# First stage of a hybrid decoder block: the modulation's weight sums as row sums on VectorE, with new step durations and margins in the kernel's own planner

## The chip, the core and the metric

The kernel runs on one core of one Trainium2 chip. The metric is the device time of one execution in microseconds (us), as the median of several runs of the same program; lower is better. The profile is one more execution with the hardware profiler on; its own device time was 1111.09 us.

## What is computed

The reference is one decoder block over a sequence of 1024 tokens with 1024 channels, all in float32. A vector `c` gives six modulation vectors of 1024 each (`mod`). The normalised input is scaled and shifted by two of them, projected to queries, keys and values, and goes through two kinds of attention side by side: mixer A, a sliding window with a sink, and mixer B, a mixture of three dilated windows. The result is projected back, gated and added; then follows an MLP with 4096 hidden channels and a squared ReLU.

```python
cond = jax.nn.silu(c)
mod = (cond @ w_ada[l] + b_ada[l]).astype(x.dtype)
sh_a, sc_a, gt_a, sh_m, sc_m, gt_m = [m[:, None, :] for m in jnp.split(mod, N_MOD, axis=-1)]

h = rms_norm(x, g_attn_pre[l]) * (1 + sc_a) + sh_a
proj = h @ w_in[l]                       # 1024 x 2304: q, k, v of both mixers
...                                      # rotary turn of the first 16 channels of each head
oa = banded_attention(qa, ka, va, A_WINDOW - 1, sink=sink_a[l])
ob = dilated_mixture_attention(qb, kb, vb)
mixed = jnp.concatenate([rms_norm(oa, g_mix_a[l]), rms_norm(ob, g_mix_b[l])], axis=-1)
y = mixed @ w_out[l]
x = x + gt_a * rms_norm(y, g_attn_post[l])

h = rms_norm(x, g_mlp_pre[l]) * (1 + sc_m) + sh_m
y = jnp.square(jax.nn.relu(h @ w_up[l])) @ w_down[l]
x = x + gt_m * rms_norm(y, g_mlp_post[l])
```

## The kernel before

**Arithmetic.** Every float32 product is made of three passes on TensorE in a rounded format: each operand is split into a high part (a copy, on ScalarE, ACT) and a low part (the original less the high part, on VectorE, DVE), and high by high, low by high and high by low are added in PSUM. So each 128x512 product step is three matmuls (L897, L898, L900 in the projections; L1799 to L1801 in the output; L2232 to L2234 in the MLP).

**The planner.** The order of all work is set while the program is built. Each piece of work is a step with a duration written in the source, the steps it depends on, the buffers it takes and gives back, and a priority. The class `Sched` keeps a clock for each of PE (TensorE), ACT, DVE, POOL (GpSimd) and SP (the DMA queue), and again and again emits the step that can start first by its own durations (`pick`, `first` and `run`, L266 to L333). The queue of each engine is then fixed in that order, whatever the chip does. A step of a higher `crit` may overtake. On TensorE, steps stand in named streams ("dense" for projections, "s", "t" and "pv" for the attention's scores, transposes and products, "post", "mod", "xt" and so on); `prefer` (L2390) lists the streams by rank, and the first stream is taken whose head is ready `SURE` microseconds before now (L155, L311). Before the change that margin is 0 for the attention's streams. Durations come from small formulas such as `t_ps(n)` (ACT from PSUM), `t_sb(n)` (ACT from SBUF) and `t_dv(n)` (DVE, L338 to L363) with constants added by hand.

**First stage (L488 to L754).** Eight blocks of `x` (128 tokens x 1024, 512 KB each) are loaded, squared and summed on ACT (`x_block`, L635), the reciprocal root is taken on POOL (L479, L481), and each block is multiplied by it (L639 ACT or L640 DVE). Each block is transposed on TensorE at once (L647), and ACT or DVE copy the eight 128x128 pieces into `xnT` (L651). The first 2048 columns of `w_ada` (8 MB) arrive as four groups of four tiles (`load_ada`, L527). DVE adds up each group with the values of `silu(c)` as per-partition scalars into a 128x512 accumulator (`mod_group`, L667 and L669), TensorE sums it over partitions by 128x1 matmuls with ones (L677), and L683 to L685 make the scale `g_a` and shift `s_a` of two channel blocks k. Then, for each k, ACT writes the high part (L706) and the full value in place (L703), and DVE the low part (L709) into `hw` (`mod_chunk`). There are eight channel blocks of 128, and two token halves x of 512.

**First projection unit (`first_unit`, L919).** The columns of `w_in` are dealt to six units; each unit has three column blocks c. Unit 0 is computed while the first stage still runs: six accumulators (`acc`, one for each x and c) are held open, and k advances as the channel blocks come; the last two k (from `AHEAD` = 6) come accumulator by accumulator, so that each can be read out in turn. Until the fourth accumulator is opened, `filler` (L907) puts matmuls on constant ones (L914) into planned idle time of TensorE. The weights come in six tiles of 256 KB for each unit, split by ACT (L561) and DVE or POOL (L566).

**Rotary tables.** DVE reduces the angles (`f_turns`, L612 to L623), ACT takes the sines (`f_sin`, L627 and L628, with a table load on each side), POOL lays them out in rows (L729 and L735), TensorE transposes them (L741), ACT scales them (L743). `evac` turns an accumulator into queries and keys (L779 to L788, L796, L799) and values (L847, L853, L861, L864).

**Attention and output.** Units 1 to 5 follow ("dense" steps on `pj`) with the attention items of the earlier units between them: scores (L1311, L1156, L1216), minimum and exponent (L1326 and L1331 and their like), transposes (L1368, L1467), products (L1403, L1502). Meanwhile POOL sums the other columns of `w_ada` (L1045 to L1050). Then eight output blocks (`out_block`, L1698) load the attention's result `o`, split it (L1741 ACT, L1742 DVE), project it, norm it and transpose it for the MLP. `front` (L1713) is run in two parts for the first two blocks, which overlap the end of the attention.

**MLP.** Seven products in place of eight (a Strassen scheme) for each of four column parts, 2688 matmuls in a row.

## Time and profile before

| what | value |
|---|---|
| median of three runs | 1109.82 us (1108.37 to 1112.75) |
| profiled execution: its own time | 1111.09 us |
| profiled execution: span from first to last instruction | 1109.3 us |
| DVE, ACT, POOL busy | 816.1, 634.2, 270.5 us |
| matmuls on TensorE | 5280 |
| first MLP matmul starts | 486.1 us |
| last MLP matmul starts | 1099.0 us |

Times in the profile are microseconds from the span's start. A busy time of TensorE counts each matmul from its start to its modelled end; matmuls overlap, so the pitch from one start to the next says more than the duration of one. "Idle before" is the time that an engine stood still ahead of an instruction, with what ended it. The views used are the page, the busy time by windows, the order of time by engine, the groups by line and shape, and the waits.

### The profile page before, as it was taken

What the parts mean: (1) busy time and instruction counts of PE and PEld (TensorE: products, weight loads), DVE (VectorE), ACT (ScalarE), POOL (GpSimd) and SP (SyncE); (2) the same over time, 40 slices, a digit from 0 to 9 for tenths busy, and PEclk for the clock granted to TensorE, in tenths of its full rate; (3) what the DMA queues carried; (4) which work ended last, traced back from release to release, by engine and by line L of the source; (5) the groups of instructions that cost most, each with busy time, mean ns of one, the idle gap of its engine ahead of it and who ended that gap; (6) DMA issues with size and microseconds to landing.
All of it is one profiled execution on the core that took longest, in us unless ns stands there. A gap on an engine that the chain in (4) does not pass through costs nothing.

```text
span 1109.3 us, 15373 instructions
## 1 busy us (share of the span) xinstructions
PE 1085.2 (98%) x5280; PEld 901.6 (81%) x5280; DVE 816.1 (74%) x1442; ACT 634.2 (57%) x1161; POOL 270.5 (24%) x365
## 2 busy tenths in 40 slices
PE   8999999999999999999999999999999999999996
PEld 6778888888888888788888888888888888888885
DVE  6968776667767778679797654898644996537998
ACT  7859776655456857677675244743155632347542
POOL 2447767587566641100000000000000000000002
PEclk9999999999999999999999999999999999999999
DMA  9665556453525537547731379322576043593104
GB/s 332 195 211 169 152 182 214 141 197 115 194 75 197 176 107 246 171 184 269 276 143 58 130 248 349 136 76 75 197 268 228 1 133 115 191 329 143 58 1 152
DMA packets 93631, 189.56 MB, mean 171 GB/s; under 512 B 8560, under 2 KB 33264, under 8 KB 93552
## 3 DMA queue, kind: packets, MB, share of 16 engines
q1 hardware_dynamic: 93552, 188.57, 49.3%
q8 instruction: 42, 0.69, 0.3%
q14 instruction: 37, 0.30, 0.1%
HBM read 139.25 MB, written 30.41 MB: 153 GB/s over the span
## 4 chain that ended last, share of the span: by engine, by line
PE 79%; DVE 8%; POOL 3%; issue 3%; ACT 3%; DMA 3%; SPq 1%; DVEq 0%; POOLq 0%; ACTq 0%
PE mlp_ps L2233 17%; PE mlp_ps L2234 17%; PE mlp_ps L2232 17%; PE pj L897 4%; PE pj L900 3%; PE pj L898 3%; PE y_ps L1799 2%; PE y_ps L1801 2%; PE y_ps L1800 2%; PE s_ps L1216 1%; PE o_ps L1502 1%; PE o_ps L1403 1%; PE s_ps L1311 1%; POOL ada_acc L1050 1%; PE pt_ps L1467 1%
## 5 line engine op out<-in xcount | busy, mean ns | idle before, releaser
L2232 PE MATMUL mlp_ps<-hw 128*128 128x512 f32 x896 | 349.6, 390 | 0.0
L2234 PE MATMUL mlp_ps<-hw 128*128 128x512 f32 x896 | 348.6, 389 | 0.0
L2233 PE MATMUL mlp_ps<-hw 128*128 128x512 f32 x896 | 348.6, 389 | 0.0
L2232 PEld LDWEIGHTS mlp_ps<-hw 128*128 128x128 f32 x896 | 168.2, 188 | 35.3 <-issue 0.5
L2233 PEld LDWEIGHTS mlp_ps<-hw 128*128 128x128 f32 x896 | 168.2, 188 | 35.3 <-issue 0.5
L2234 PEld LDWEIGHTS mlp_ps<-hw 128*128 128x128 f32 x896 | 168.2, 188 | 34.9
L2000 DVE TENSOR_TENSOR hw<-w,hw 128x1024 fp32r<-128x1024 f32 x94 | 112.3, 1221 | 94.0 <-ACT hw L1993 93.7
L1993 ACT CAST hw<-w 128x1024 fp32r<-128x1024 f32 x94 | 95.5, 1049 | 129.8 <-PE mlp_ps L2234 93.1
L2332 POOL TENSOR_TENSOR st<-st,nhalf 128x1 f32<-128x1 f32 x8 | 7.8, 983 | 610.2 <-DVE st L2330 610.2
L897 PE MATMUL pj<-hw,w_hl 128*128 128x512 f32 x240 | 102.7, 428 | 2.0 <-ACT vt L847 2.0
L900 PE MATMUL pj<-hw,w_hl 128*128 128x512 f32 x240 | 94.7, 395 | 0.0
L898 PE MATMUL pj<-hw,w_hl 128*128 128x512 f32 x240 | 94.5, 394 | 0.0
L1993 ACT CAST hw<-u 128x1024 fp32r<-128x1024 f32 x48 | 48.7, 1052 | 64.5 <-PE mlp_ps L2234 64.5
L2000 DVE TENSOR_TENSOR hw<-u,hw 128x1024 fp32r<-128x1024 f32 x48 | 57.1, 1220 | 18.2 <-ACT hw L1993 18.2
L2290 DVE TENSOR_TENSOR yacc<-yacc,mlp_ps 128x512 f32<-128x512 f32 x96 | 62.2, 683 | 3.3 <-PE mlp_ps L2234 3.3
L1050 POOL TENSOR_TENSOR ada_acc<-ada_acc,wa_st 128x512 f32<-128x512 f32 x42 | 55.5, 1321 | 3.5
L900 PEld LDWEIGHTS pj<-hw,w_hl 128*128 128x128 f32 x240 | 45.2, 188 | 10.4
L1799 PE MATMUL y_ps<-hw,oh 128*128 128x512 f32 x128 | 51.9, 405 | 0.4 <-ACT y_sb L1817 0.4
L897 PEld LDWEIGHTS pj<-hw,w_hl 128*128 128x128 f32 x240 | 45.4, 189 | 6.0 <-ACT vt L847 2.2
L1800 PE MATMUL y_ps<-hw,oh 128*128 128x512 f32 x128 | 49.9, 390 | 0.0
L898 PEld LDWEIGHTS pj<-hw,w_hl 128*128 128x128 f32 x240 | 45.7, 190 | 3.8 <-issue 0.2
L2271 ACT ACTIVATE u<-u 128x512 f32<-128x512 f32 x48 | 29.0, 625 | 32.9 <-DVE u L2269 32.4
(257 smaller groups left out, 1992.8 us busy)
## 6 DMA issues: line engine op xcount, KB each, us to landing
hw<-s_dram SPq DMA_DIRECT2D x84, 512.0 KB, 4.2
wa_st<-in_w_ada SPq DMA_DIRECT2D x32, 512.0 KB, 4.6
w<-in_w_up SPq DMA_DIRECT2D x32, 512.0 KB, 4.7
w<-in_w_down SPq DMA_DIRECT2D x32, 512.0 KB, 7.1
s_dram<-hw SPq DMA_DIRECT2D x28, 512.0 KB, 3.7
qt<-hl SPq DMA_DIRECT2D x40, 256.0 KB, 2.5
w_st<-in_w_in SPq DMA_DIRECT2D x36, 256.0 KB, 2.9
x_sb<-in_x SPq DMA_DIRECT2D x16, 512.0 KB, 5.7
```

Source lines behind the costliest of these rows:

```text
L897: T.matmul(ps, w[:, 0, n], h[0], start=(k == 0), stop=False)
L898: T.matmul(ps, w[:, 1, n], h[0], start=False, stop=False)
L900: T.matmul(ps, w[:, 0, n], h[1], start=False, stop=(k == KC - 1))
L1050: G.tensor_tensor(ada.acc[:, :512], ada.acc[:, :512], wa[:, j], ALU.add)
L1799: T.matmul(ps[:], oh, wh[:, c0:c0 + 512], start=(k == 4 * m), stop=False)
L1800: T.matmul(ps[:], oh, wl[:, c0:c0 + 512], start=False, stop=False)
L1993: A.copy(out[j][0], flat(src[j]))
L2000: V.tensor_tensor(out[j][1], flat(src[j]), out[j][0].bitcast(F32), ALU.subtract)
L2232: T.matmul(ps[m][:], sh, mh, start=starts and k == 0, stop=False, **kw)
L2233: T.matmul(ps[m][:], sh, ml_, start=False, stop=False, **kw)
L2234: T.matmul(ps[m][:], sl, mh, start=False, stop=k == 3, **kw)
L2290: e = op("DVE", t_dv(512), lambda: V.tensor_tensor(y(), y(), ps[m][:], ALU.add), [e, ml.e_y[tb, n]], gives=gives, prio=1)
```

## The change

Four things are changed.

1. **The first stage.** The host hands over the first 2048 columns of `w_ada` a second time, transposed (`w_mod`: for each channel block k and each of shift and scale, 128 output channels on partitions by 1024 inputs). `silu(c)` is spread to all partitions: DVE makes a diagonal, TensorE sums it with ones (two matmuls), the result `condb` is copied to SBUF. Each element of `g_a` and `s_a` is then one row sum on DVE: 16 `tensor_tensor_reduce` of 128x1024 take the place of the accumulation and of the 128x1 matmuls. The blocks of `x` stay in eight buffers of their own; they are transposed only when channel block k is wanted, four token blocks at a time, and ACT reads high part and full value straight from PSUM. `xnT` and its copies are gone. The loads are in another order: four blocks of `x`, the two tiles of k = 0, a tile of `w_in`, the other four blocks of `x`, and then two tiles for each k. From x block 4 on DVE may do the square as well. The sine's table is loaded at the start, the exponent's after k = 2.
2. **Durations.** Some thirty durations in the planner's steps are set anew, most of them longer.
3. **Margins.** `SURE` is 0.3 for the attention's streams and "post". The last `xn` of one output block waits for that of the block before.
4. **First output blocks.** The split of `o` of blocks 0 and 1 has `crit` 1, and the two loads of one block stand in order.

```diff
-SURE = dict(s=0.0, t=0.0, pv=0.0, post=0.0, fin=1.0)
+SURE = dict(s=0.3, t=0.3, pv=0.3, post=0.3, fin=1.0)
...
+    w = inputs["w_ada"][0][:, :2 * D].reshape(P, KC, 2, KC, P)
+    h["w_mod"] = np.ascontiguousarray(w.transpose(3, 2, 4, 1, 0)).reshape(KC, 2, P, D)
...
 def t_ps(n):
-    return 0.055 + 0.00083 * n
+    return 0.12 + 0.00083 * n
 def t_sb(n):
-    return 0.098 + 0.00083 * n
+    return 0.16 + 0.00083 * n
...
-    order0 = [("x", 0), ("x", 1), ("x", 2), (0, 0), (0, 1), ("x", 3), (0, 2), ("w", 0), (0, 3), ("w", 1)]
+    order0 = [("x", 0), ("x", 1), ("x", 2), ("x", 3), (0, 1), (0, 0), ("w", 0)]
     order0 += [("x", t) for t in range(4, TB)]
+    for k in range(1, KC):
+        order0 += [(k, 1), (k, 0)] + {1: [("w", 1)], 2: [("w", 2)], 3: [("w", 3)], 4: [("w", 4)], 5: [("w", 5)]}.get(k, [])
...
+    e_sin = op("ACT", 1.5, lambda: A.activation(small.tile([P, 8], F32, name="rs_t", tag="rs_t")[:, 0:1], ones[:, 0:1],
+                                                AF.Sin), [e, e_init], prio=0)
...
+        V.tensor_tensor(by_k(bc["diag"]), ident.unsqueeze(1).to_broadcast([P, KC, P]),
+                        cond[:].unsqueeze(2).to_broadcast([P, KC, P]), ALU.mult)
...
+            T.matmul(bc[n][:], ones[:], bc["diag"][:, 512 * n:512 * n + 512], start=True, stop=True)
...
+        def dot(i, dst):
+            w = wa_t[k, i][:]
+            V.tensor_tensor_reduce(w, w, condb[:], 1.0, bb[:, k, i:i + 1], ALU.mult, ALU.add, dst[:, k:k + 1])
...
-                        V.scalar_tensor_tensor(b["acc"][:], w, cj, b["acc"][:], ALU.mult, ALU.add)
...
-                    T.matmul(b["ps"][:, k, i:i + 1], b["acc"][:, GW * i + k * P:GW * i + k * P + P], ones[:, 0:1],
-                             start=True, stop=True)
...
+        bank, tag, r_b = (px, "x", r_x) if half else (pt, "t", r_t)
+            for j in range(4):
+                T.transpose(b["ps"][:, j], x_t[4 * half + j][:, ks], ident)
+        eh = op("ACT", t_ps(512) + AP_COST, lambda: A.activation(hh, b["ps"][:], AF.Identity, bias=s_a[:, k:k + 1],
+                                                                    scale=g_a[:, k:k + 1]), [d] + e_ada[k], prio=0)
+            A.activation(b["h"][:], b["ps"][:], AF.Identity, bias=s_a[:, k:k + 1], scale=g_a[:, k:k + 1])
+        e = op("DVE", t_dv(512), lambda: V.tensor_tensor(hl, b["h"][:], hh.bitcast(F32), ALU.subtract), [eh, e],
+               gives=[(r_h, 1)], prio=0)
...
-            e = op("POOL", 4.0, f_rows, [e_rope], takes=[(r_place, 1)], prio=0)
+            e = op("POOL", 8.0 if r_place is r_wa else 4.4, f_rows, [e_rope], takes=[(r_place, 1)], prio=0)
...
-        e = op("DVE" if eng is V else "POOL", 1.2 if eng is V else 3.64, f_acc,
+        e = op("DVE" if eng is V else "POOL", 1.4 if eng is V else 4.1, f_acc,
...
-        e = op("DVE", 0.2, f_z, ex, prio=0)
+        e = op("DVE", 0.62, f_z, ex, prio=0)
...
-            el = load(f_lo, 262144 * n, deps, takes=[] if m0 else [(r_o_, 1)], prio=-8.5 if tb == 0 else -6)
+            el = load(f_lo, 262144 * n, deps + eo.get("ld", []), takes=[] if m0 else [(r_o_, 1)],
+                      prio=-8.5 if tb == 0 else -6)
+            eo["ld"] = [el]
...
-            e = op("ACT", t_sb(512 * n), f_oh, [el], takes=[(r_g[m0], n)], prio=2)
+            e = op("ACT", t_sb(512 * n), f_oh, [el], takes=[(r_g[m0], n)], prio=2, crit=int(early))
```

How this moves the queues is seen at three places. The first is TensorE from the program's first matmul on: `acc<-ones_r` are fillers, `pxt<-head,x_sb` the transposes of `x`, `acc<-hw,w_hl` the first real projections. Before:

```order
L914 MATMUL acc<-ones_r 128x512 x26
L647 MATMUL pxt<-head,x_sb 128x128 x8
L914 MATMUL acc<-ones_r 128x512 x2
L647 MATMUL pxt<-head,x_sb 128x128 x8
L914 MATMUL acc<-ones_r 128x512
L647 MATMUL pxt<-head,x_sb 128x128 x8
L914 MATMUL acc<-ones_r 128x512 x10
L647 MATMUL pxt<-head,x_sb 128x128 x8
L914 MATMUL acc<-ones_r 128x512 x3
L677 MATMUL pm<-ones,acc_a 128x1 x4
L914 MATMUL acc<-ones_r 128x512 x5
L897 MATMUL acc<-hw,w_hl 128x512
```

TensorE from the same place in the changed kernel (`pbc` is the spread of `silu(c)`):

```order
L909 MATMUL acc<-ones_r 128x512 x15
L609 MATMUL pbc<-diag,ones 128x512
L909 MATMUL acc<-ones_r 128x512
L609 MATMUL pbc<-diag,ones 128x512
L909 MATMUL acc<-ones_r 128x512 x25
L691 MATMUL pxt<-head,x_sb 128x128 x4
L909 MATMUL acc<-ones_r 128x512 x8
L892 MATMUL acc<-hw,w_hl 128x512
L893 MATMUL acc<-hw,w_hl 128x512
L909 MATMUL acc<-ones_r 128x512
```

Ahead of the first real matmul stood 32 transposes and four 128x1 matmuls (and 47 fillers); now four transposes, two `pbc` and 49 fillers stand there, and the other transposes come between the projections. In the whole program there are 61 fillers in place of 60, 64 transposes of `x` as before, and no `pm`.

The second place is DVE in the middle of the first stage. Before, two channel blocks came at a time, after a run of accumulations:

```order
L709 TENSOR_TENSOR hw<-xnT,hw 128x8x128 x2
L669 SCALAR_TENSOR_TENSOR acc_a<-wa,cond,acc_a 128x512 x4
L683 TENSOR_TENSOR g_a<-pm,bb 128x2
L684 TENSOR_TENSOR g_a<-g_a,head 128x2
L685 TENSOR_TENSOR s_a<-pm,bb 128x2
L669 SCALAR_TENSOR_TENSOR acc_a<-wa,cond,acc_a 128x512 x2
L566 TENSOR_TENSOR w_hl<-w_st,w_hl 128x512
```

DVE in the changed kernel, where `ISA wa,g_a<-wa,condb,bb` is one row sum and the row after it reads its accumulator:

```order
L672 ISA wa,g_a<-wa,condb,bb 128x1024
L672 ISA g_a 128x1
L676 TENSOR_TENSOR g_a<-g_a,head 128x1
L700 TENSOR_TENSOR hw<-h,hw 128x4x128 x2
L563 TENSOR_TENSOR w_hl<-w_st,w_hl 128x512
L672 ISA wa,s_a<-wa,condb,bb 128x1024
L672 ISA s_a 128x1
```

Each channel block now has two row sums of its own, and the low parts (L700, before L709) stand between them in pieces of half the size.

The third place is ACT around the first copy of values of unit 1, `vt<-pj` (`p_sb,den` are the attention's exponents, `ph<-pt_ps` copies of transposed probabilities, `otmp` copies of an attention result). Before:

```order
L1331 ACTIVATE p_sb,den_1258<-p_sb,mn_1257 128x257 x4
L1331 ACTIVATE p_sb,den_1323<-p_sb,mn_1322 128x257 x2
L796 ACTIVATE hl<-pj 64x512
L1331 ACTIVATE p_sb,den_1323<-p_sb,mn_1322 128x257 x2
L1438 COPY otmp<-o_ps 64x512
L1375 CAST ph<-pt_ps 128x512 x2
L847 COPY vt<-pj 64x512
L561 CAST w_hl<-w_st 128x512
```

ACT around the same copy in the changed kernel:

```order
L1326 ACTIVATE p_sb,den_1166<-p_sb,mn_1165 128x257 x2
L1370 CAST ph<-pt_ps 128x512 x2
L1326 ACTIVATE p_sb,den_1166<-p_sb,mn_1165 128x257 x2
L791 ACTIVATE hl<-pj 64x512
L1433 COPY otmp<-o_ps 64x512
L842 COPY vt<-pj 64x512
L1370 CAST ph<-pt_ps 128x512 x2
L1326 ACTIVATE p_sb,den_1288<-p_sb,mn_1287 128x257
```

Between `hl<-pj` and `vt<-pj` five instructions stood before, two exponents among them; now it is one.

More of the change, by code (lines that the diff above doesn't have):

```diff
@@ L117, in _host @@
     h["consts"] = c
-    return h
+    return {n: h[n] for n in _INS + ["consts"]}
 def _constants(c):
@@ L714, in hybrid_block @@
     for tb in range(TB):
         x_block(tb)
-    for g in range(4):
-        mod_group(g)
-    e = op("ACT", 3.2, f_sin, [e_ang] + e_xn[0] + e_xn[1], prio=8)
-    e_rope = op("DVE", 0.15, lambda: V.tensor_scalar(sinw[:, :, 0], sinw[:, :, 1], -1.0, None, ALU.mult), [e],
-                prio=8)
+    for k in range(KC):
+        ada_chunk(k)
+    for k, half in [(k, x) for k in range(KC) for x in range(2)]:
+        if half == 0 and k < 6:
+            split_w(0, k)
+        mod_chunk(k, half)
@@ L1193, in part @@
             return f
-        eq = op(("ACT", "POOL"), (t_as(1024), 1.5), (part(A.copy), part(G.tensor_copy)), e_q[u, 1], takes=[(r_qf, 1)],
+        eq = op(("ACT", "POOL"), (2.0, 2.03), (part(A.copy), part(G.tensor_copy)), e_q[u, 1], takes=[(r_qf, 1)],
                 prio=3)
```

213 lines of the change are left out of this document (94 added, 119 removed).

## Prediction

> **What bounds the kernel now.** I read the page first, for who is last.
>
> ```profile
> PE 1085.2 (98%) x5280; PEld 901.6 (81%) x5280; DVE 816.1 (74%) x1442; ACT 634.2 (57%) x1161; POOL 270.5 (24%) x365
> PE 79%; DVE 8%; POOL 3%; issue 3%; ACT 3%; DMA 3%; SPq 1%; DVEq 0%; POOLq 0%; ACTq 0%
> ```
>
> TensorE (PE) is busy in 98% of the span and carries 79% of the chain that ended last. So a change pays only where PE stands still, or runs matmuls that compute nothing. The busy time by windows (PE, PEld, DVE, ACT and POOL in us, granted clock, DMA share, GB/s) shows where that is.
>
> ```profile
> 0.00:10.00 10.00, 8.49 (x31) 6.88 (x32) 6.60 (x33) 5.74 (x8) 1.82 (x8) 1.00 0.76 254
> 10.00:20.00 10.00, 7.82 (x52) 6.32 (x50) 7.66 (x12) 7.18 (x15) 3.16 (x4) 1.00 1.06 391
> 20.00:30.00 10.00, 9.33 (x49) 7.25 (x48) 7.08 (x14) 9.33 (x16) 3.99 (x8) 1.00 1.08 358
> 30.00:40.00 10.00, 8.55 (x48) 6.87 (x49) 9.48 (x18) 10.00 (x15) 0.95 (x1) 1.00 0.89 283
> 500.00:600.00 100.00, 100.00 (x445) 82.84 (x443) 87.76 (x94) 66.18 (x93) 0.00 (x0) 1.00 0.55 205
> ```
>
> In the MLP (the last window) PE never waits, and the diff does not touch its steps. In the first 40 us PE looks busy for 34.2 of 40 us, but the order of time on PE and its groups of the first 80 us show with what.
>
> ```profile
> 1.50 8.12 PE L914 MATMUL acc<-ones_r 128*128 128x512 f32 x26 [1.50 <-DVE nhalf L591]
> 22.00 0.50 PE L897 MATMUL acc<-hw,w_hl 128*128 128x512 f32 x1 [0.46 <-ACT hw L706]
> 34.62 0.48 PE L914 MATMUL acc<-ones_r 128*128 128x512 f32 x1
> 40.17 0.39 PE L897 MATMUL acc<-hw,w_hl 128*128 128x512 f32 x1
> 42.66 0.39 PE L898 MATMUL acc<-hw,w_hl 128*128 128x512 f32 x1
> 68.37 0.39 PE L900 MATMUL acc<-hw,w_hl 128*128 128x512 f32 x1
> L914 PE MATMUL acc<-ones_r 128*128 128x512 f32 x60 | 19.1, 446 | 1.5 <-DVE nhalf L591 1.5
> L647 PE MATMUL pxt<-head,x_sb 128*128 128x128 f32 x64 | 8.6, 278 | 3.0 <-ACT x_sb L639 1.6 <-ACT xnT L651 1.4
> ```
>
> The first real matmul starts at 22.00, the last filler (a matmul on ones) at 34.62, the last matmul of unit 0 at 68.37. Twelve matmuls start from 40.17 to 42.66, eleven pitches of 0.227 us, which is the price of one real matmul. Unit 0 has 144 of them: 32.7 us. The stage is therefore late by its inputs and not by its work.
>
> After the first stage I took the waits of PE between 70 and 500 us (total, times, longest).
>
> ```profile
> PE pj L897 <- ACT vt L847: 2.0, 1, 2.0
> PE ada_ps L1066 <- POOL ada_acc L1050: 1.5, 2, 1.3
> PE x_far L1252 <- DVE z_far L1245: 0.9, 1, 0.9
> PE ada_ps L1063 <- POOL ada_acc L1050: 0.2, 1, 0.2
> ```
>
> These are the first three and the last of twelve rows, which add up to 8.4 us. The longest costs more than its 2.0, as the windows round it and PE's rows show.
>
> ```profile
> 109.50:120.00 10.50, 9.44 (x49) 7.61 (x49) 8.52 (x21) 6.25 (x14) 8.55 (x11) 0.84 0.74 221
> 107.57 1.04 PE L1368 MATMUL pt_ps<-head,p_sb 128*128 128x128 f32 x8
> 110.56 0.50 PE L897 MATMUL pj<-hw,w_hl 128*128 128x512 f32 x1 [1.96 <-ACT vt L847]
> ```
>
> The granted clock is 0.84 over the 10.5 us behind this wait: 0.16 x 10.5 = 1.7 us of full clock lost. So 10.1 us hang on waits and clock between 70 and 500.
>
> **The first stage after the change, step by step.** All loads come on one queue, and at 358 to 391 GB/s (windows above) 512 KB take 1.4 us. The first block of x is there at 5.37, where ACT begins its square.
>
> ```profile
> 5.37 1.06 ACT L635 ACTIVATE junk<-x_sb 128x1024 bf16<-128x1024 f32 x1 [1.82 <-DMA x_sb<-in_x]
> L743 ACT ACTIVATE tab<-ptab,head 128x512 f32<-128x512 f32 x8 | 5.5, 688 | 2.1 <-PE ptab L741 2.1
> L639 ACT ACTIVATE x_sb<-x_sb,rstd 128x1024 f32<-128x1024 f32 x4 | 4.6, 1148 | 2.1 <-POOL rstd L481 2.1
> L481 POOL TENSOR_TENSOR rstd<-rs_t,nhalf 128x1 f32<-128x1 f32 x8 | 5.9, 735 | 0.7
> ```
>
> In the new order of loads x3 lands at about 9.6, the two tiles of k = 0 at 11.0 and 12.4, the first weights at 13.1, x7 at 18.7, the tiles of k = 1 at 20.1 and 21.5, and then a pair with its weights each 3.5 us, so k = 7 at about 42. ACT does four squares (1.06 each with the sum's read), two copies of `condb` (0.53), one product with the root (1.05): 5.37 + 6.4 = 11.8; then the sines (0.4, when DVE has the angles at about 11.2), the first weights (from 13.1, 0.6) and x3 times its root (1.05), at 14.8. Ahead of the first high part stand two more squares in ACT's queue, of x4 and x5; x5 lands at 15.9, so the high part is done at 17.7. I take 17.8 for the first real matmul, 4.2 us before today's 22.00.
>
> From there three engines run beside each other. DVE has these prices:
>
> ```profile
> L669 DVE SCALAR_TENSOR_TENSOR acc_a<-wa,cond,acc_a 128x512 f32<-128x512 f32 x28 | 20.9, 751 | 1.3 <-DMA wa<-in_w_ada 0.8
> L667 DVE TENSOR_SCALAR acc_a<-wa,cond 128x512 f32<-128x512 f32 x4 | 1.9, 482 | 0.0
> L1168 DVE CUSTOM_DVE_ANT_0 p_sb<-s_ps,masks 128x512 f32<-128x512 f32 x8 | 5.5, 681 | 1.5 <-PE s_ps L1156 1.5
> L1168 DVE CUSTOM_DVE_ANT_0 p_sb<-s_ps,masks 128x256 f32<-128x256 f32 x8 | 3.3, 416 | 0.1
> L709 DVE TENSOR_TENSOR hw<-xnT,hw 128x512 fp32r<-128x512 f32 x4 | 2.7, 689 | 0.6 <-ACT xnT L703 0.6
> 57.05 2.36 DVE L709 TENSOR_TENSOR hw<-xnT,hw 128x1024 fp32r<-128x1024 f32 x2 [2.87 <-ACT xnT L703]
> ```
>
> The old sums cost 28 x 0.751 + 4 x 0.482 = 23 us. `tensor_tensor_reduce` stands in the trace on smaller tiles (L1168): 681 - 416 = 265 ns for 256 elements, so a row of 1024 is 681 + 2 x 265 = 1211 ns, and with the bias operand and the accumulator's read about 1.3. Sixteen are 21 us, and eight small products 0.6: nearly what goes. Two copies to `xnT` go from DVE (1.4), the diagonal comes (1.2). Per k DVE has 2 x 1.3 for sums, 2 x 0.62 for low parts (0.69 less the overlap with the next) and 0.62 for weights: 4.6 us. From the landing of k = 1 at 20.1 the order gives DVE 14 sums, 16 low parts, 5 weight splits and some 0.8 us of small things, 33 us without a gap, which ends at 53; the last low part waits for ACT's two last pairs and comes at 54.4. Today the last pair of L709 starts at 57.05 and ends at 59.4.
>
> ACT has per k four passes of 128x512 from PSUM at the 688 ns of L743, less overlap 0.6 to 0.65, and 0.55 for weights: 3.1 us, below DVE.
>
> PE: the first low part of k = 0 needs ACT's full value, which stands behind two squares (x6, x7) and a product and ends at 21.6, and then one DVE step: 22.8. PE waits for it. The last filler falls at about 23.5. Behind it the order holds 135 real matmuls (30.7 us), 13 groups of four transposes (64 of L647 are 8.6 us of busy time, 0.54 a group with its drain; I take 0.45, 5.9 us) and 16 table transposes (1.7): 61.8. I add 0.6 for the last low part of k = 7 on DVE, which PE reaches a little early: 62.4, so 8.0 behind DVE's last, against 68.6 today (68.37 and a pitch). **The stage gives 6.2 us.** What hides the extra transposes and the two `pbc` matmuls is idle time of PE, which fillers hold otherwise.
>
> Its bounds: PE's queue is in order, and the transposes of the second half use one PSUM buffer that ACT must empty twice before the next. If each k loses 0.5 us there, 4 us go and 2.2 stay. Upward, if ACT does the first high part before x5 lands (the order forbids it) or the low parts are early, 9 us.
>
> The sine's table is loaded at the start and the exponent's after k = 2, where both stood in a row with ACT idle else.
>
> ```profile
> 42.46 1.28 ACT L627 ACT_TABLE_LOAD   x1
> 43.76 0.26 ACT L627 ACTIVATE sinw<-ang 128x64 f32<-128x64 f32 x1
> ```
>
> A load takes 1.28 and the next instruction starts 0.02 behind it. The new one starts at 3.55, behind the exponent of `c`, and ends at 4.85, hidden by the wait for x0 until 5.37. [...]
>
> The rotary turn on DVE waits today:
>
> ```profile
> 64.02 0.69 DVE L779 TENSOR_TENSOR hl<-acc,tab 64x512 f32<-64x512 f32 x1 [3.41 <-ACT tab L743]
> ```
>
> It starts at 64.0, behind the table from ACT. With sines at 12 and POOL's rows done long before, it waits for PE's table transposes only, which stand among the last real matmuls, and comes at about 57. So the attention moves with PE.
>
> **Durations and margins.** Real work on PE is the same but for order. Between 70 and 500 us the change acts on 10.1 us of waits and clock. The worst place is one that the new order mends: PE's projections stood behind `vt`, and that copy behind two exponents and three copies in ACT's queue; now one copy stands between. I take the 3.7 us (2.0 and 1.7) as gone. The other 6.4 are short waits of 0.2 to 1.3 on results that the plan held ready too soon. New durations are near the trace, as these rows for steps now set to 2.03 and 0.74 show:
>
> ```profile
> L1192 POOL CAST q_far<-qt 128x1024 fp32r<-128x1024 f32 x6 | 12.2, 2036 | 6.8 <-PE s_ps L1216 5.8 <-DMA qt<-hl 1.0
> L1841 POOL TENSOR_TENSOR st<-rs_t,nhalf 128x1 f32<-128x1 f32 x14 | 10.4, 744 | 58.3 <-DVE rs_t L1839 58.3
> ```
>
> I let 2 of the 6.4 go and add 1.7 for new waits that another order makes, so the part gives **4.0 us**. No row shows what a margin does, so the bounds are wide: all 10.1 gained at best, and 4 lost at worst (one more wait like the one at 110, with its clock). The split of o of blocks 0 and 1 sooner is worth at most the 0.8 of one of the twelve rows and is in this.
>
> **Sum.** 1111.1 of the profiled execution less 6.2 and 4.0 is 1100.9. That execution is 1.3 above the median 1109.8, so the median should be 1099.6.
>
> **Rivals.**
> Only one half comes (A). PE loses 4 us at the one PSUM buffer and DVE is late, so the stage gives 2.2, and the attention 2: 1105.6, within 0.5%. For it: PE is in order and DVE and ACT run at 4.6 and 3.1 us a k against PE's 5.0 (18 x 0.227 and 0.85), so slack is thin. Against it: the plan now has the true durations.
> The order mends nearly all waits (B): 9 and 10.1 gained, 1090.7. For it speaks that each wait is short; against it that 12 rows of waits have 12 different places, and one order seldom mends all.
> The margin costs (C): a step of the attention now lets a projection of 0.68 us go first unless its input is 0.3 us old by the plan; if this delays ACT and DVE, waits only move and two more like that at 110 appear: 7.4 lost against 6.2 gained, 1111. Against: the same count of projections is left at each point of PE's work in both orders.
> Slower, by the row sums (D): the trace has no `tensor_tensor_reduce` with two operands in SBUF that writes in place. If one took 2.4 us and not 1.3, DVE, which is without a gap from 20 us on, would end 16 x 1.1 = 17.6 us later, at 72.0, and unit 0 8.0 behind it, at 80.0: 11.4 lost, less 4.0 for the attention, is 1117.2. It decides from 1.7 us a sum, where the stage gives nothing. For it: only PSUM rows bound it. Against: L669, with two operands in SBUF, has 751 for 512, no more per element than L1168.
> The clock too might fall in the first stage, where PE waits 1.8 us for the first low part: 1.7 us as at 110; this is in the range. [...]
>
> **How the numbers follow.** Forecast 0.62, A 0.15, B 0.08, C 0.09, D 0.06. A measurement of this kernel can tell about 0.5% (5.5 us) from no change. Faster by more: the forecast and B, 0.70. Within: A and most of C (0.07) and a little of D (0.01), 0.23. Slower: D (0.05) and the rest of C (0.02), 0.07. The range reaches from B's 1091 to 1108, past A; above it lie C and D.
>
> **What would show it.** Right: the first real matmul near 18, the last low part near 54, the last `acc` matmul near 62, row sums of 1.2 to 1.3 us, a sine load that ends before 5.4, no wait on `vt` near 103, and PE's waits from 65 to 490 below 6 us. Wrong: gaps on PE ahead of `pxt` or of the matmuls on low parts, row sums above 1.7, a clock below 1 in the first 60 us, or waits of PE in the attention as long as now.

## The result, and the profile after

| kernel | median us (range) | runs | profiled execution: its time, span |
|---|---|---|---|
| before | 1109.91 (1108.37 to 1113.06) | 6 | 1111.09, 1109.3 |
| changed | 1101.65 (1101.32 to 1104.14) | 6 | 1103.07, 1101.3 |

The ratio is 0.9932, with a 95% interval of 0.9914 to 0.9951: the change makes the kernel 0.7% faster, 8.2 us by the medians and 8.0 by the two profiled executions. Page of the changed kernel, busy time of each engine and the chain of work that ended last:

```profile
PE 1080.8 (98%) x5253; PEld 900.6 (82%) x5253; DVE 805.5 (73%) x1428; ACT 624.5 (57%) x1163; POOL 287.2 (26%) x379
PE 88%; DVE 4%; ACT 2%; POOL 2%; issue 2%; DMA 2%; SPq 0%; DVEq 0%; POOLq 0%; ACTq 0%
```

TensorE's share of the chain rose from 79% to 88%. Its busy time by windows, in the same columns as before:

```profile
10.00:20.00 10.00, 7.76 (x32) 5.68 (x31) 6.15 (x15) 8.11 (x15) 5.50 (x9) 0.91 1.03 412
20.00:30.00 10.00, 9.85 (x50) 7.88 (x49) 8.38 (x15) 8.69 (x15) 2.93 (x5) 0.92 0.77 285
30.00:40.00 10.00, 10.00 (x53) 8.28 (x52) 9.93 (x20) 7.78 (x12) 4.09 (x8) 1.00 0.96 358
500.00:600.00 100.00, 100.00 (x443) 82.80 (x442) 84.73 (x84) 63.18 (x85) 0.00 (x0) 1.00 0.52 193
```

The granted clock falls to 0.91 and 0.92 in the first stage, where it was 1.00 before. PE's order of time in the changed kernel shows the gap ahead of that, the first real matmul, and the first matmul of unit 1 (`pj`), which stands right behind unit 0:

```profile
16.70 0.33 PE L691 MATMUL pxt<-head,x_sb 128*128 128x128 f32 x1 [2.16 <-ACT x_sb L662]
19.44 0.79 PE L892 MATMUL acc<-hw,w_hl 128*128 128x512 f32 x1
65.16 0.39 PE L892 MATMUL pj<-hw,w_hl 128*128 128x512 f32 x1
478.67 0.39 PE L2230 MATMUL mlp_ps<-hw 128*128 128x512 f32 x1
```

The same two steps of before, the first matmuls of unit 1 and of the MLP:

```profile
68.60 0.39 PE L897 MATMUL pj<-hw,w_hl 128*128 128x512 f32 x1
486.14 0.39 PE L2232 MATMUL mlp_ps<-hw 128*128 128x512 f32 x1
```

This cuts the gain in three. Unit 0 ends 68.60 - 65.16 = 3.4 us sooner. From there to the MLP it takes 413.5 us in place of 417.5, 4.0 less. The remaining 0.6 of the 8.0 lies behind. These are single executions; what others say of the 3.4 stands under the experiments. PE's waits in the changed kernel between 70 and 490 us, the first three and the last of ten rows, which add up to 7.2 us:

```profile
PE pm_o L1754 <- DVE o_sb L1748: 3.1, 2, 1.7
PE s_ps L1211 <- DVE st_far L1226: 1.7, 1, 1.7
PE pm_o L1754 <- DVE ph L1478: 0.5, 1, 0.5
...
PE y_ps L1796 <- DVE y_sb L1820: 0.2, 1, 0.2
```

The wait on `vt` is gone, and with it its low clock. But from the end of unit 0 to the MLP the sum of the waits hardly fell, from 7.9 to 7.2. They moved in time: up to 330 us they were 5.2 us and are 0.6, and behind 330 us, where the first output blocks begin and few projections are left to fill gaps, they were 2.7 and are 6.6. The three long ones there (1.42, 1.72 and 1.67 us) leave the clock at 1.00, while the 1.96 on `vt` had cost 1.7 us of clock.

The clock was not gained, though. In the changed kernel it falls once in this stretch as well, at another place: behind a wait of only 0.44 us and eight narrow matmuls (128x1). PE's rows there, and the windows:

```profile
189.96 1.19 PE L1211 MATMUL s_ps<-kt,q_far 128*128 128x128 f32 x8 [0.44 <-POOL q_far L1187]
190.97 0.97 PE L1061 MATMUL ada_ps<-ones,ada_acc 128*128 128x1 f32 x8
190.00:195.00 5.00, 5.00 (x27) 4.37 (x28) 1.32 (x11) 2.18 (x10) 3.63 (x4) 0.73 0.37 112
195.00:200.00 5.00, 5.00 (x30) 4.38 (x30) 4.08 (x8) 1.65 (x3) 4.83 (x5) 0.93 0.00 0
```

That is (0.27 + 0.07) x 5 = 1.7 us, as much as behind `vt`. So waits account for 0.7 of the 4.0 us and the clock for nothing. The other 3.3 lie in PE's work between the waits, which has the same matmuls in another order; no view here shows where, and that stays open.

Why the first matmul came at 19.44 and not at 17.8 stands in the order of time on POOL: the two small steps of the root of x3, and the product on ACT that waits for them.

```profile
12.80 0.92 POOL L482 TENSOR_SCALAR rs_t<-ssq 128x1 f32<-128x1 f32 x1 [1.15 <-ACT junk L654]
13.80 1.66 POOL L484 TENSOR_TENSOR rstd<-rs_t,nhalf 128x1 f32<-128x1 f32 x1
15.50 1.15 ACT L662 ACTIVATE x_sb<-x_sb,rstd 128x1024 f32<-128x1024 f32 x1 [1.89 <-POOL rstd L484]
```

For another block, with no row sum beside them, the same two steps take 0.22 and 0.57 (17.77 and 18.08). Beside these ones DVE ran its first two row sums:

```profile
12.36 1.28 DVE L672 CUSTOM_DVE_ANT_0 wa<-wa,condb,bb 128x1024 f32<-128x1024 f32 x1
13.76 1.28 DVE L672 CUSTOM_DVE_ANT_0 wa<-wa,condb,bb 128x1024 f32<-128x1024 f32 x1
```

The sums end at 13.56 and 14.96, 1.20 behind their starts, where their accumulators are read; POOL's steps end at 13.72 and 15.46, each behind the sum beside it.

### The profile page after: what moved, and what is told of

It is laid out like the page before. It is cut to its first block, busy times and chain, and to the rows that moved or that the text cites. A ratio compares the mean times of both kernels' runs of the same rounds, so it can differ in the third digit from the quotient of the medians.

```text
span 1101.3 us, 15270 instructions
## 1 busy us (share of the span) xinstructions
PE 1080.8 (98%) x5253; PEld 900.6 (82%) x5253; DVE 805.5 (73%) x1428; ACT 624.5 (57%) x1163; POOL 287.2 (26%) x379
## 4 chain that ended last, share of the span: by engine, by line
PE 88%; DVE 4%; ACT 2%; POOL 2%; issue 2%; DMA 2%; SPq 0%; DVEq 0%; POOLq 0%; ACTq 0%
PE mlp_ps L2230 18%; PE mlp_ps L2232 18%; PE mlp_ps L2231 18%; PE pj L892 5%; PE pj L895 4%; PE pj L893 4%; PE y_ps L1796 2%; PE y_ps L1798 2%; PE y_ps L1797 2%; PE s_ps L1306 1%; PE s_ps L1211 1%; PE o_ps L1497 1%; PE o_ps L1398 1%; PE pt_ps L1363 1%; PE acc L895 1%
```

## The experiments

Twelve kernels, each timed beside the kernel before. Each has line numbers of its own. The first stage's end is the start of the first `pj` matmul; the stretch goes from there to the first MLP matmul; the waits are those of PE in the stretch, in all and up to 330 us. The last column counts how often the granted clock fell in the stretch; in the traces of the kernel before (from 111.44 to 114.85) and of the changed kernel (from 192.27 to 195.68) a fall is 3.41 us at a granted clock of 0.50, so 1.7 us lost, and a window of 5 us at 0.66, as other runs have it, loses as much (0.34 x 5).

| kernel | ratio to before (95%) | stage ends | stretch | waits, to 330 | falls |
|---|---|---|---|---|---|
| before | 1 | 68.6 | 417.5 | 7.9, 5.2 | 1 |
| changed | 0.9932 (0.9914 to 0.9951) | 65.2 | 413.5 | 7.2, 0.6 | 1 |
| stage_alone | 1.0029 (1.0014 to 1.0044) | 65.6 | 421.5 | 11.3, 8.5 | 2 |
| plan_alone | 0.9994 (0.9979 to 1.0009) | 67.5 | 417.6 | 10.1, 5.2 | 1 |
| no_margin | 0.9974 (0.9957 to 0.9990) | 66.3 | 416.3 | 9.7, 4.4 | 0 |
| old_dur | 0.9984 (0.9967 to 1.0001) | 65.9 | 416.9 | 9.3, 1.0 | 1 |
| no_crit | 0.9976 (0.9961 to 0.9990) | 65.8 | 418.7 | 9.8, 0.8 | 3 |
| margin_20 | 0.9948 (0.9929 to 0.9967) | 66.1 | 412.7 | 6.6, 1.1 | 0 |
| margin_40 | 1.0027 (1.0010 to 1.0043) | 66.6 | 420.5 | 12.9, 5.4 | 1 |
| sums_behind_root | 0.9923 (0.9901 to 0.9945) | 64.1 | 412.2 | 7.1, 0.7 | 0 |
| both_behind_root | 0.9923 (0.9903 to 0.9943) | 65.3 | 410.4 | 5.6, 0.7 | 0 |
| gap_filled | 0.9953 (0.9936 to 0.9971) | 66.2 | 413.8 | 7.3, 1.6 | 1 |
| qfar_act | 0.9962 (0.9946 to 0.9979) | 66.2 | 413.0 | 7.8, 1.6 | 0 |
| root_margin_25 | 0.9969 (0.9954 to 0.9984) | 65.4 | 421.6 | 11.1, 6.0 | 3 |

The stretch less its waits and less 1.7 us for each fall is 403.8 to 407.9 us in all fourteen, so waits and falls together make most of the differences in it. From before to changed it went from 407.9 to 404.6; these are the 3.3 us above.

How far one profiled execution can be trusted is the next question. With the first stage's order unchanged, the first real matmul came at 19.44 to 20.86 in eight executions, and the changed kernel's was the earliest. What sets it stands at the program's start: `pbc`, the spread of `silu(c)`, stands behind 15 fillers in PE's queue. PE's rows in the changed kernel, and then in `margin_40`:

```profile
1.50 5.08 PE L909 MATMUL acc<-ones_r 128*128 128x512 f32 x15 [1.50 <-DVE nhalf L589]
6.42 1.02 PE L609 MATMUL pbc<-diag,ones 128*128 128x512 f32 x2
1.50 6.56 PE L909 MATMUL acc<-ones_r 128*128 128x512 f32 x15 [1.50 <-DVE nhalf L589]
7.90 1.02 PE L609 MATMUL pbc<-diag,ones 128*128 128x512 f32 x2
```

These fillers start 0.43 us apart at first and 0.23 apart later, and the step between the two comes at another time in each execution, at 4.6 us in the first and 7.7 in the second. ACT copies `pbc` into `condb` between its squares of `x`, so it waits for it. This is the copy in the changed kernel and in `qfar_act`, where x0's square began sooner (at 5.42 and not 5.92) and the wait was longer:

```profile
7.48 0.59 ACT L612 COPY condb<-pbc 128x512 f32<-128x512 f32 x1 [0.41 <-PE pbc L609]
8.61 0.59 ACT L612 COPY condb<-pbc 128x512 f32<-128x512 f32 x1 [2.04 <-PE pbc L609]
```

Counted from the start of `pbc`, the executions agree: in these eight and in `gap_filled` the first real matmul comes 12.95 to 13.02 us later and the first stage ends 58.66 to 58.85 later. So the 65.2 of the changed kernel is the lucky end of 65.2 to 66.6. The old stage ended at 68.6 and, in `plan_alone`, at 67.5, and the stage's gain is 1.0 to 3.4 us by these executions.

With the order of every queue the same but for one or two tiny copies, the stretch took 413.5, 412.2 and 410.4; 1.7 us of that spread is the fall at 192 us, which only the first has.

**Each half alone.** `stage_alone` is the changed kernel with the later steps' old durations, no margin and the old loads and split of `o`; `plan_alone` is the kernel before with the new ones.

```diff
-SURE = dict(s=0.3, t=0.3, pv=0.3, post=0.3, fin=1.0)
+SURE = dict(s=0.0, t=0.0, pv=0.0, post=0.0, fin=1.0)
...
+def t_ps0(n):
+    return 0.12 + 0.00083 * n
...
 def t_ps(n):
-    return 0.12 + 0.00083 * n
+    return 0.055 + 0.00083 * n
```

> The changed kernel with its new first stage, but with the old durations of all later steps, no margin, and o split and loaded as before. Theory (two halves that add up): the first stage ends 4.1 us sooner as in the changed kernel (the last acc matmul near 64.3 against 68.4), the waits of PE from 62 to 480 us are those of before (about 8 us, with one of 2 us on vt and a clock below 1 behind it), and the time is 1109.9 - 4.1 = 1105.8. Rival 1 (the stage is all): 1101.7, with the order of the attention worth nothing. Rival 2 (the stage shifts the attention against its loads, so that the old order fits worse): above 1107.

> The kernel before with its old first stage, and only the later steps' new durations, the margin of 0.3, and o split sooner. Theory (two halves that add up): the first stage ends as before (last acc matmul near 68.4), the wait on vt and the low clock behind it are gone, and the time is 1109.9 - 3.9 = 1106.0. Rival 1 (the stage is all): 1109.9. Rival 2 (the durations only fit together with the new stage): 1108 to 1112, with new waits of 2 us in the attention.

Alone, the new stage makes the kernel slower by 0.3% although it ends sooner, and the new plan alone changes nothing that can be measured. PE's waits where the stage was changed alone, the two longest:

```profile
PE pv L856 <- ACT vt L850: 3.8, 1, 3.8
PE pv L856 <- DVE gate_st L1083: 3.7, 1, 3.7
```

Behind the first of them the clock falls to 0.66 (a window of the same run), and the second stands behind a step of DVE at the head of its queue that waits 5.81 us for a load (DVE's order of time):

```profile
135.00:140.00 5.00, 5.00 (x20) 4.16 (x19) 3.19 (x12) 2.67 (x9) 1.28 (x4) 0.66 0.81 256
```

```profile
167.08 0.69 DVE L1083 TENSOR_TENSOR gate_st<-ada_ps,gate_st 128x512 f32<-128x512 f32 x1 [5.81 <-DMA gate_st<-in_b_ada]
```

Where the plan was changed alone, the long wait stands at another place (PE's order of time), and the clock falls behind it too (window):

```profile
78.51 1.08 PE L1319 MATMUL s_ps<-kt,qt 128*128 128x128 f32 x8 [2.06 <-DMA kt<-hl]
```

```profile
80.00:85.00 5.00, 5.00 (x21) 4.20 (x19) 2.89 (x15) 2.79 (x12) 1.41 (x2) 0.66 0.90 244
```

The theory of two halves that add up falls, and so does the rival that the stage is all. Rival 2 of both stands (for `plan_alone` it is the new wait of 2.06 us that speaks for it; its time fits rival 1 as well): the order of the attention fits, or does not fit, the times at which its inputs come, and the stage sets these. By the ratios the halves give +3.2 and -0.7 us and both together -7.5: the 10 us between are the fit of the two.

**Parts of the plan, on the new stage.** `no_margin` sets the four margins to 0; `old_dur` puts back the old durations alone; `no_crit` leaves out the rule for the split of `o`, in this step and in the one behind it:

```diff
-            e = op("ACT", t_sb(512 * n), f_oh, [el], takes=[(r_g[m0], n)], prio=2, crit=int(early))
+            e = op("ACT", t_sb(512 * n), f_oh, [el], takes=[(r_g[m0], n)], prio=2)
```

> The changed kernel with all margins of the attention at 0, as before; new stage, new durations and the sooner split of o stay. Theory (the durations make the order fit the new stage): no wait of PE of 2 us or more between 62 and 200 us, and the time within 2 us of the changed kernel's 1101.7. Rival 1 (the margin does it): one or two waits of 2 to 4 us with a clock below 1 behind them, as where the stage was changed alone, and 1106 to 1112. Rival 2 (the margin costs): 1099 or less.

> The changed kernel with the old durations for all steps behind the first stage; new stage, margin of 0.3 and the sooner split of o stay. Theory (the durations make the order fit the new stage): the plan again holds copies ready too soon, one or two waits of 2 to 4 us between 62 and 200 us with a clock below 1 behind them, and 1107 to 1112. Rival (the margin does it): no such wait, and 1101 to 1103.

> The changed kernel without the rule that lets the split of o of the first blocks go ahead on ACT and DVE; all else stays. Theory (that split costs: a step of 2.13 us on DVE stands ahead of the far minima, and PE waits 1.7 us for st_far and 1.4 and 1.7 for o_sb): PE's loss from 340 to 420 us, 11.6 us in the changed kernel, falls to about the 8 of the kernel before, and the time is 1098 to 1100. Rival 1 (it costs nothing, the waits come from elsewhere): the same waits stay, 1101.7. Rival 2 (it helps as meant): other waits of over 2 us from 340 to 420, 1103 or more.

Taking any one of the three away costs about as much (0.4 to 0.5%), and in three different ways. Without the margin the waits come back before 330 us (4.4 us). With the old durations these stay away and the late ones grow: waits on `o_sb` of 5.1 us in all. Without the rule for `o` there are two waits of 3.3 us on results of DVE, of which the second is the very split that came too late, and the clock falls three times (windows of 5 us at 0.66, at 0.81 and 0.85, and at 0.75 and 0.91):

```profile
377.50 0.60 PE L1247 MATMUL x_far<-z_far,masks 128*128 128x32 f32 x4 [3.34 <-DVE z_far L1240]
422.99 0.80 PE L1798 MATMUL y_ps<-hw,ol 128*128 128x512 f32 x1 [3.31 <-DVE ol L1739]
```

So my theory of `no_crit`, that the sooner split costs time, was wrong: it helps as meant (rival 2). In the other two the times are those of rival 1 of `no_margin` (1107.1) and of the theory of `old_dur` (1108.8), but without the waits of 2 to 4 us ahead of 200 us that were to make them, so neither expectation fits as a whole.

**Is the margin a mechanism?** `margin_20` and `margin_40` change one number, and the last run, `root_margin_25`, sets 0.25 together with the edit of the next paragraph.

```diff
-SURE = dict(s=0.3, t=0.3, pv=0.3, post=0.3, fin=1.0)
+SURE = dict(s=0.4, t=0.4, pv=0.4, post=0.4, fin=1.0)
```

> The changed kernel with a margin of 0.2 in place of 0.3 for the four kinds of attention steps. Theory 1 (the margin is a mechanism: the more of it, the fewer steps come before their input): between the 1101.7 of 0.3 and the 1107.1 of 0, near 1103.5, with waits before 200 us between 0.4 and 4.4. Theory 2 (any change of the plan makes another order, with one or two long waits at places that the value doesn't tell): 1105 to 1109, with one or two waits of over 2 us or a place before 330 us where PE stands for 2 us or more.

> The changed kernel with a margin of 0.4 in place of 0.3 for the four kinds of attention steps. Theory 1 (the margin is a mechanism): PE's idle time before 330 us stays below 1 us, and the time is 1100 to 1103. Theory 2 (any change of the plan makes another order): 1105 to 1109, with one or two waits of over 2 us.

> The changed kernel with the sums of k = 0 held behind the root of x3 (1.0 us faster when done alone) and a margin of 0.25 in place of 0.3. Theory 1 (from 0 to 0.3 the margin works evenly, 1107.1, 1103.2 and 1101.7, so that 0.25 costs at most 1): 1100 to 1102. Theory 2 (each value makes another order, and 0.4 showed that one more wait of 2.8 us at a new place decides): 1104 to 1110 with such a wait, or, if the draw is good and PE's idle time is below 6 us in all between 66 and 480 us, 1098 to 1099, faster than both kernels and than the run with the sums held alone.

For margins of 0, 0.2, 0.25, 0.3 and 0.4 the ratios are 0.9974, 0.9948, 0.9969, 0.9932 and 1.0027 (the third together with the edit of the next paragraph, which alone makes the stage shorter). That is no even effect: 0.25 is slower than 0.3, by intervals that part, and by its value slower than 0.2 too, where they overlap a little; 0.4 is slower than no margin at all. PE's longest wait with 0.4, and then with 0.25:

```profile
141.09 1.19 PE L1306 MATMUL s_ps<-kt,qt 128*128 128x256 f32 x4 [2.83 <-DMA o_dram<-ot]
```

```profile
136.50 0.66 PE L761 MATMUL ptab<-head,rows 128*128 128x128 f32 x4 [2.28 <-ACT tab L763]
```

Each value makes another order, and one wait of over 2 us with its clock (0.66 over 5 us behind the 2.83, 0.71 and 0.95 over 5 us each behind the 2.28), at a place that the value does not tell, weighs most with 0.25 and 0.4. Theory 2 of `margin_40` and `root_margin_25` stands, though `margin_40` came out slower than its 1105 to 1109 (1112.2); `margin_20` alone had looked like theory 1, and its ratio can't be told from that of the changed kernel.

**The row sums beside POOL.** `sums_behind_root` puts a copy of one element on DVE ahead of the two sums of k = 0, and issues these behind the root of x3. `both_behind_root` does the same for k = 1 and x7.

```diff
+            if then:
+                V.tensor_copy(small.tile([P, 8], F32, name="rs_t", tag="rs_t")[:, 0:1], dst)
+                then()
```

> The changed kernel with one edit: a one-element copy on DVE that reads the root of x3 stands ahead of the two row sums of k = 0, so that no row sum runs while POOL computes that root. Theory (POOL's two small steps are slowed by the row sums beside them, 0.92 and 1.66 us against 0.22 and 0.57 elsewhere): the two steps take 0.25 and 0.6, x3's product starts at 13.7 and not at 15.5, the first real matmul comes at 17.7 and not at 19.4, the last filler 1.5 to 2 us sooner, and the time is 1100. Rival 1 (POOL is slow there for another reason): the steps stay at 0.9 and 1.7, the sums move behind 15.5, the first real matmul comes at about 20 and the time is 1102 to 1103. Rival 2 (DVE sets the end of the stage and not the start of PE): the first matmul is sooner but the last low part stays near 55.8, and the time is 1101.7.

> As the run with the sums of k = 0 held behind the root of x3, and the two sums of k = 1 are held in the same way behind the root of x7, which there took 0.77 and 1.50 us beside such a sum; the order of everything else is that of the changed kernel. Theory (the row sums slow POOL's small steps, and the first low part waits for x7 through them): the steps for x7 take 0.22 and 0.57, its product starts at about 20.2 and not at 21.55, the last filler comes near 24 and not at 24.9, and the time is 1099.5 to 1100. Rival (the sums of k = 1 are themselves what is late next): the last filler stays at 24.9 or later, the last low part comes later by the 0.5 us for which the sums are held, and the time is 1100.7 to 1101.5.

With the sums of k = 0 held, POOL, ACT and PE in the order of time:

```profile
12.87 0.22 POOL L482 TENSOR_SCALAR rs_t<-ssq 128x1 f32<-128x1 f32 x1 [1.20 <-ACT junk L667]
13.17 0.57 POOL L486 TENSOR_TENSOR rstd<-rs_t,nhalf 128x1 f32<-128x1 f32 x1
13.78 1.15 ACT L675 ACTIVATE x_sb<-x_sb,rstd 128x1024 f32<-128x1024 f32 x1 [0.19 <-POOL rstd L486]
17.73 0.50 PE L917 MATMUL acc<-hw,w_hl 128*128 128x512 f32 x1 [0.56 <-ACT hw L718]
64.11 0.39 PE L917 MATMUL pj<-hw,w_hl 128*128 128x512 f32 x1
```

The steps begin at the same time as in the changed kernel (12.87 against 12.80) and take 0.22 and 0.57: the first real matmul comes 1.7 us sooner, unit 0 ends 1.05 sooner. Counted from `pbc`, the first real matmul comes after 11.23 to 11.24 us in the three executions with these sums held, where it was 12.95 to 13.02, and the stage ends after 57.62 here and 57.64 in `root_margin_25`, where it was 58.66 to 58.85. The cause is shown, and its price at the stage's end is 1.0 to 1.2 us. The medians, 1100.70 and 1101.65, agree with it, but the two intervals overlap. The steps of 0.77 and 1.50 us, which the expectation of `both_behind_root` takes for x7's, are x6's; those of x7 stand behind them in POOL's queue. With the sums of k = 1 held as well, x6's second step took 0.57 and x7's root came 0.9 us sooner, measured from x3's steps, but the first stage did not end sooner (65.25, with x3's steps 0.8 later in this execution, is 64.4 beside 64.1): the product of x7 now stood on DVE behind the held sum. For the stage the rival's result came, by a way that neither had named.

**The clock in the first stage.** `gap_filled` puts eight matmuls on ones into the gap ahead of x3.

```diff
+                if k == half == 0 and j == 3:
+                    for _ in range(8):
+                        T.matmul(accs[FILL][:], ones_r[:, :P], ones_r[:], start=True, stop=True)
```

> The changed kernel with eight more matmuls on ones between the third and the fourth transpose of x for k = 0, where PE stands still for 2.2 us ahead of x3; nothing else. Theory: the gap is filled, the granted clock of the first 30 us is 1.00 and not 0.91 and 0.92, but the time stays within 0.5 us of the changed kernel's 1101.7, since fillers run until 26 us in any case and the first low part waits for ACT and DVE. Rival (the low clock is what the first stage lost): 1.7 us faster, 1100.0. If the clock stays at 0.91 with the gap filled, a gap of 2.2 us isn't what lowers it.

The windows of the filled kernel have the full clock:

```profile
10.00:20.00 10.00, 9.69 (x44) 7.34 (x42) 5.31 (x14) 8.08 (x17) 5.08 (x9) 1.00 1.03 409
20.00:30.00 10.00, 9.11 (x45) 6.97 (x45) 7.81 (x15) 8.70 (x14) 3.88 (x6) 1.00 0.71 261
```

Its `pbc` came 1.10 us later in this execution (7.52 against 6.42), its stage ended 1.04 later, and the stretch is the same, with one fall as well. From `pbc` to the stage's end it took 58.68 us against 58.74: filling the gap gained nothing that can be seen, as the theory has it, since PE runs fillers there until 26 us. The median is 2 us above that of the changed kernel, in another set of runs and with overlapping intervals, so a small loss is not excluded. And the gap alone does not lower the clock: `stage_alone` has the same gap (2.15 us) at the same place and six other runs have one of 2.08 to 2.10, and the clock stayed at 1.00 in all seven.

**DVE beside POOL in the attention.** `qfar_act` issues the eight copies to `q_far` on ACT; the other queues are unchanged.

```diff
-        eq = op(("ACT", "POOL"), (2.0, 2.03), (part(A.copy), part(G.tensor_copy)), e_q[u, 1], takes=[(r_qf, 1)],
+        eq = op(("ACT", "POOL"), (2.0, 2.03), (part(A.copy), part(A.copy)), e_q[u, 1], takes=[(r_qf, 1)],
```

> The changed kernel with the eight copies of q for the far blocks, each about 2.05 us on POOL, issued on ACT at the same places of the order; every other queue is the same. Theory (DVE's steps with two inputs in SBUF stand still while POOL works: the low part of o at 369 took 2.13 us in place of 0.68 beside such a copy): that step takes 0.7, PE's wait of 1.7 us for st_far becomes less than 0.6, and, if ACT has room for 2 us at each place, the time is 1100. Rival (ACT has no room): the step on DVE is short, but exponents come later, new waits of 1 to 3 us on ACT's results appear, and the time is 1103 to 1107. If the step stays at about 2 us, POOL's copy isn't what slows it.

In the changed kernel, the copy on POOL and the low part of `o` on DVE, which the minima for `st_far` follow:

```profile
368.75 2.01 POOL L1187 CAST q_far<-qt 128x1024 fp32r<-128x1024 f32 x1
369.19 2.13 DVE L1739 TENSOR_TENSOR oh<-o_sb,oh 128x512 fp32r<-128x512 f32 x1 [1.16 <-ACT oh L1737]
```

The same step with the copies on ACT, and PE's wait near it:

```profile
368.72 0.68 DVE L1739 TENSOR_TENSOR oh<-o_sb,oh 128x512 fp32r<-128x512 f32 x1
372.69 0.50 PE L1796 MATMUL y_ps<-hw,oh 128*128 128x512 f32 x1 [1.67 <-ACT y_sb L1814]
```

The step takes 0.68, and PE's 1.72 us for `st_far` are gone; 1.67 us on ACT have come in their place, and the kernel is no faster. That POOL's copy slows the step is shown. The changed kernel's trace also fits the two inputs in SBUF that the theory names: L700, with both there, took 1.77 us at 52.80, beside a POOL step of 2.29, and 0.69 in most of its 16, while L1374, with one input in PSUM, took 0.54 to 0.69 in all its 54, those beside POOL among them. Moving the copies only moved the wait, as the rival has it (1106.3, in its 1103 to 1107).

## Why the prediction was right or wrong, point by point

**Where the time was predicted right.** 1099.6 against 1101.65, inside the range and faster by over 0.5%. The two terms were 6.2 and 4.0; measured are 3.4, 4.0 and 0.6 elsewhere, and the 3.4 is the upper end of what the executions show (1.0 to 3.4).

**The stage's term was too large, and the step that failed is ACT's sum up to the first matmul.** The step "x3 times its root (1.05), at 14.8" let ACT go on to the product as soon as the first weights were split: the wait for POOL's root of x3, and what row sums beside it do to that root, stood at nothing. In the changed kernel POOL's two steps took 2.66 us from start to end, where they take 0.87 with the sums held; ACT waited 1.89 for them, the product ended at 16.65, and the first matmul came 1.64 late. Of the 2.8 us that unit 0 ended late (65.16 for 62.4), this is 1.05, by the run with the sums held. There the first matmul came at 17.73, as forecast, although x0's square began at 5.79 and not 5.37, so the start of the loads is no part of it.

For the remaining 1.7 the same omission is the candidate, one step on. "ACT's full value" was to end at 21.6 behind "two squares (x6, x7) and a product", again without POOL. In the run with the sums of k = 0 held, ACT waits for x6's root there, whose second step took 1.50 us beside the third sum:

```profile
21.55 1.15 ACT L675 ACTIVATE x_sb<-x_sb,rstd 128x1024 f32<-128x1024 f32 x1 [1.80 <-POOL rstd L486]
```

The full value ends at 23.37, and the last filler comes at 24.94 for 23.5. The run with both pairs of sums held put another step in the way, so this stays open. Behind the last filler the sum was right: 39.1 us to the end in the changed kernel, where 38.9 were forecast. ACT's wait for `pbc` stood at nothing too; it is 0.41 us in this execution, but in others it moves the whole stage by up to 1.5.

Two slips in DVE's sum change nothing, because the last low part was put behind ACT: the terms per k add up to 4.5 and not 4.6 us, and those from 20.1 on to 32.0 and not 33.

**Row sums, tables, rotary turn.** The groups by line of the first 80 us:

```profile
L672 DVE CUSTOM_DVE_ANT_0 wa<-wa,condb,bb 128x1024 f32<-128x1024 f32 x16 | 20.4, 1277 | 0.0
```

1.28 for the 1.3 estimated from two smaller shapes, so rival D fell. The last low part starts at 55.79 and ends at 56.5, 2.1 later than the 54.4 predicted, where the last filler was 2.5 late. The sine's table load ended at 5.36, the next instruction began 0.02 behind it, and x0's square, at 5.92, waited 0.33 for its own load: here the table's load was hidden, as forecast. The rotary turn came at 59.9, not 57; no listed wait of PE up to 330 us hangs on it.

**The clock.** It did fall in the first stage (0.50 from 18.19 to 21.60), which the prediction held "in the range", but behind the gap of 2.16 us ahead of x3's transpose, and not where PE was to wait for the first low part. By the run with the gap filled it cost the end under 0.1 us.

**The attention's term had the right size and the wrong reason.** `vt` was mended, as said. But another fall of the clock came at 192 us, the waits are 7.2 us where the prediction's sign asked for under 6, and waits and clock hold only 0.7 of the 4.0. The step "I let 2 of the 6.4 go and add 1.7" treated the waits as single items of which a better plan mends some. The runs show in its place that the whole stretch is another order each time: the same plan on the old stage gives nothing, the old plan on the new stage loses 4.0 us, and 0.1 more of margin costs 11 us, where 0.1 less costs nothing that can be told. That the sum of the terms came out at -8 is the fit of this stage with this margin. A prediction from this trace could say that the stretch would lie somewhere between 410 and 422 us; the 4.0 inside that was luck. The chance of 0.23 for a time within 0.5% of before was too low: eight other orders gave stretches of 412.7 to 421.6, and seven of these kernels lie within 0.5% of before, none slower by more.

**Rivals.** A's mechanism (the one PSUM buffer) was not seen: the stage was late from its start and not by k. B did not come, since waits moved to behind 330 us. C's two more waits "like that at 110" did not come with 0.3; one came with 0.4, and two where the stage was changed alone, without any margin.

## What to carry to other kernels

Where a planner writes fixed queues, edits do not add: time the halves apart and together, and take a margin or a duration as a draw, to be tried at several values, because one or two waits of over 2 us, and each fall of the clock (1.7 us here), can outweigh all the small waits. When work is moved to DVE, look at what POOL does beside it: here a tiny step of POOL on the critical path took about as long as the long DVE instruction that ran with it (1.66 us beside one of 1.28, and 0.57 without). A view of the waits by stretch, ahead of and behind the point where the fillers run out, shows whether waits have gone or only moved; count the falls of the clock beside them. And before the time of a stage in one profiled execution is trusted, look for a step that stands behind fillers at the program's start: here `pbc` behind 15 of them moved the whole stage by up to 1.5 us. Taking it ahead of them was not tried.

## What the runs showed of the hardware

POOL and DVE held each other up. Beside a row sum POOL's steps of 128x1 took 0.92 and 1.66 us, and 0.22 and 0.57 without it; beside POOL's cast of 2.01 us a DVE subtraction of 128x512 took 2.13, and 0.68 without it. In both cases the slowed step ends 0.16 to 0.6 us behind the end of the other. What the two share was not shown.

The granted clock fell to 0.66 over 5 us (0.34 x 5 = 1.7 us lost) behind waits of PE of 2.06 and 3.76 us and, with 0.4, of 2.83, and not behind 1.42, 1.67 and 1.72. But it also fell behind a wait of 0.44 with eight 128x1 matmuls of 0.97 us in all, so the length of the wait alone does not decide. A gap of 2.08 to 2.16 us at one place lowered it in one execution of eight. The lost 1.7 us is 3.41 us at a granted clock of 0.50 in the traces of the kernel before and of the changed kernel, behind waits of 1.96 and of 0.44.

At the program's start 128x512 matmuls on ones followed each other every 0.43 us, and every 0.23 from a time on that was between 4.5 and 7.7 us in the nine executions with the new stage's order; the windows show a granted clock of 1.00 on both sides.
